# The samples' attention of a hybrid decoder step: bias by VectorE, two visits per chunk, seven value buffers

## The chip, the cores and the metric

The kernel runs on one core of a Trainium2 chip. The time is that of one execution on the device in microseconds; several executions are taken and their median is given. The profile is one more execution, recorded by the hardware profiler.

## The reference, cut to what matters

One layer of a decoder works on two groups that share all weights: a prompt of 2048 tokens, and 8 samples of 8 new tokens each, which look back at 8192 cached tokens. What matters here is the samples' attention over the cache:

```
kp = cache_k[l][page_table]          # 8 samples x 8192 tokens x 8 heads x 64
a  = lfp - reverse_cumsum(lfp)       # bias of each cached token and head
s  = q . k * scale + lq - lk         # lk = [a, lnew]
p  = softmax(where(k_pos <= q_pos, s, -inf))
o  = p . v
```

Everything is float32. The rest of the layer (projections of 8200 columns, pooling, a short convolution, the prompt's own attention, three branch products, gates, the output product, a norm) is not touched.

## The kernel before, in words

The program has three phases on TensorE. Phase 1 (`phase1`) computes all projections of the 2112 tokens: each group of 128 output columns has its weights loaded (`load_w`, line 325), split into a high and a low part (lines 326 and 327), and multiplied with the two parts of the normed input in three products for each of 8 row blocks (lines 350 to 352), in chunks of 512, 256 and 320 or 512 columns. Phase 2 is the prompt's attention, with branch products between its steps. Phase 3 is the output product.

The samples' attention (`decode`) is a Python generator that runs in the background of phase 1: after each projection chunk, `pump` takes as many steps of it as the columns done so far call for. A scheduler then orders every engine's instructions by a timeline of its own; the order of the code sets priorities. Only inside phase 2 is TensorE's order written out by hand.

Before it starts, `decode_bias` gathers the log forget values of the cache in four parts, sums them along the tokens, and stores the bias to DRAM as two arrays `s_nbh` and `s_nbl`, a high and a low part in the reduced format of TensorE's fast products. `decode_consts` makes `sel`, a matrix of zeros and ones.

A sample has 8 chunks of 8 pages (1024 tokens), 64 chunks in all. For each chunk, in four steps between which the generator yields:

1. Two loads bring the chunk's bias, `nbt`, from `s_nbh` and `s_nbl` (line 952). Two gathers bring keys, `kg` (two buffers, issued by GpSimd, line 923), and VectorE transposes them into `kt` (one buffer, line 959). Into one PSUM bank, `dS`, go two selection products, `sel` with `nbt`, which spread the bias over the rows (line 964), and on top 16 score products (line 969), each in a quarter of the columns of the array.
2. VectorE takes the maximum over both halves (line 974) and negates it (line 976); ScalarE takes the exponential and its sum (line 979); TensorE transposes the result (line 985), and ScalarE copies it to `pT` (line 988).
3. Eight products of `pT` with the first four tiles of values, `v` (line 995); the four gathers for the next tiles are put behind them (`values`, line 923).
4. Eight more with the next four tiles; VectorE masks and reduces the sum (lines 1008 and 1010).

`v` has four buffers, as many as one step uses. The first product of a step reads the tile that is gathered last:

```
with self.tc.issue_after(product(0, 3).ins):
    for x in (0, 1, 2, 4, 5, 6, 7):
        product(x // 4, x % 4)
```

GpSimd issues all gathers from one queue, and SP nearly all other transfers, both in order.

Of the kernel before, what the change touches and what calls it, by code (L numbers as in the profile page):

```python
# [8 lines left out]
F32 = mybir.dt.float32  # L9
F32R = mybir.dt.float32r  # L10
I32 = mybir.dt.int32
U32 = mybir.dt.uint32
# [6 lines left out]
P = 128  # L19
# [20 lines left out]
class Mixer:  # L40
# [5 lines left out]
    def pools(self):  # L46
# [15 lines left out]
        self.s_nbh = dt("s_nbh", [NB * NPG, NH, P])  # L62
        self.s_nbl = dt("s_nbl", [NB * NPG, NH, P])
# [3 lines left out]
    def setup(self):  # L67
# [12 lines left out]
        self.ks = self.dp.tile([P, 4, NS], F32, name="ks")  # L80
        self.vs = self.dp.tile([NS, BW], F32, name="vs")
# [772 lines left out]
    def decode_consts(self):  # L854
        nc, dp = self.nc, self.dp

        sel = self.stage("sel")[0:64, 0:256].rearrange("p (a b) -> p a b", b=P)
        self.sel = dp.tile([64, 2, P], F32R, name="sel")
        for part in range(2):
            q = slice(32 * part, 32 * part + 32)  # L860
            nc.gpsimd.iota(sel[q], pattern=[[4, 2], [1, 4], [8, 4], [0, 8]], base=0, channel_multiplier=-1,
                           allow_small_or_imprecise_dtypes=True)
        nc.vector.tensor_scalar(out=self.sel, in0=sel, scalar1=0.0, scalar2=None, op0=ALU.is_equal)

# [3 lines left out]
        for g in range(4):  # L868
# [12 lines left out]
        nc.gpsimd.affine_select(out=self.tri, in_=self.tri, pattern=[[-1, P]], compare_op=ALU.is_gt, fill=0.0,  # L881
                                base=0, channel_multiplier=1)
        nc.vector.memset(self.tri[64:128, 0:64], 0.0)

    def decode_bias(self):
# [3 lines left out]
        nc.sync.dma_start(idxl, I["page_table"].rearrange("(n b) g -> (b g) n", n=4).bitcast(U32))  # L889
# [3 lines left out]
        for n in range(4):  # L893
# [18 lines left out]
            hi, lo = self.stage(f"nbh{n}", F32R)[:, 0:1024], self.stage(f"nbl{n}", F32R)[:, 0:1024]  # L912
            nc.scalar.copy(hi, nb)
            V.tensor_tensor(out=lo, in0=nb, in1=hi.bitcast(F32), op=ALU.subtract)
            for d, x in ((self.s_nbh, hi), (self.s_nbl, lo)):
                nc.sync.dma_start(d[n * P : (n + 1) * P].rearrange("n h t -> n (h t)"), x.bitcast(F32))

    def decode(self):

# [5 lines left out]
        NC = 8  # L925

# [9 lines left out]
        vs = values(0)  # L936
        qbd = dp.tile([P, 16, 32], F32, name="qbd")
        nc.gpsimd.memset(qbd, 0.0)
        for b in range(NB):
# [6 lines left out]
            stat = dp.tile([P, 2, 2, NC], F32, tag="stat", bufs=2, name=f"stat{b}")  # L946
            ob = dp.tile([P, 2, HD, NC], F32, tag="ob", bufs=1, name=f"ob{b}")
            for c in range(NC):
# [4 lines left out]
                kt = dp.tile([P, 2, 2048], F32, tag="kt", bufs=1, name=f"kt{b}_{c}")  # L953
                for i in range(2):
                    kg = dp.tile([P, 2048], F32, tag="kg", bufs=2, name=f"kg{b}_{c}_{i}")
                    t = b * 16 + c * 2 + i
                    ind(kg, ck, self.idxk[:, t : t + 1])
                    for x in range(2):
                        V.transpose(out=kt[:, i, x * D : (x + 1) * D], in_=kg[:, x * D : (x + 1) * D])  # L959
                ktv = kt.rearrange("p i (j x r) -> p i j x r", j=4, r=32)  # L960
                S = self.psum("dS")
                Sv = S.rearrange("p (a i x) -> p a i x", a=2, x=P)
                for hh in range(2):
                    nc.tensor.matmul(Sv[:, hh], self.sel[:, hh], nbt, start=(hh == 0), stop=False)
                for hh in range(2):
                    for dh in range(2):
                        for h4 in range(4):
                            x = (4 * hh + h4) * 2 + dh
                            nc.tensor.matmul(Sv[32 * h4 : 32 * h4 + 32, hh], qbd[:, x], ktv[:, :, :, x],  # L969
                                             start=False, stop=(hh == 1 and dh == 1))  # L970
                yield
                S3 = S.rearrange("p (a x) -> p a x", a=2)
                m, l = stat[:, 0, :, c], stat[:, 1, :, c]
                V.tensor_reduce(out=m, in_=S3, axis=AX.X, op=ALU.max)
                nm = dp.tile([P, 2], F32, tag="nm", bufs=2, name=f"nm{b}_{c}")
                V.tensor_scalar(out=nm, in0=m, scalar1=-1.0, scalar2=None, op0=ALU.mult)
                pr = dp.tile([P, 2, 256], F32, tag="pr", bufs=1, name=f"pr{b}_{c}")
                for hh in range(2):
                    nc.scalar.activation(out=pr[:, hh], in_=S3[:, hh], func=AF.Exp, bias=nm[:, hh : hh + 1],
                                         accum_out=l[:, hh : hh + 1])  # L980
                pt = self.psum("dT")
                for hh in range(2):
                    for i in range(2):
                        x = hh * 2 + i
                        nc.tensor.transpose(out=pt[:, x * P : (x + 1) * P], in_=pr[:, hh, i * P : (i + 1) * P],
                                            identity=self.ident)
                pT = dp.tile([P, 4, 4, 32], F32, tag="pT", bufs=1, name=f"pT{b}_{c}")
                nc.scalar.copy(pT.rearrange("p x g (h q) -> p x h g q", q=NQ),
                               pt.rearrange("p (x h g q) -> p x h g q", x=4, h=4, g=4))
                yield  # L990
                O = self.psum("dO")
                for i in range(2):

                    def product(hh, g):
                        return nc.tensor.matmul(O[32 * g : 32 * g + 32, hh * 256 : hh * 256 + 256],  # L995
                                                pT[:, 2 * hh + i, g], vs[g][:, hh * 256 : hh * 256 + 256],
                                                start=(i == 0 and hh == 0), stop=(i == 1 and hh == 1))


                    with self.tc.issue_after(product(0, 3).ins):  # L1000
                        for x in (0, 1, 2, 4, 5, 6, 7):
                            product(x // 4, x % 4)
                    if (b * NC + c) * 2 + i + 1 < NB * NC * 2:
                        vs = values((b * NC + c) * 2 + i + 1)
                    if i == 0:
                        yield
# [577 lines left out]
```

## Time and profile before

| | us |
|---|---|
| runs before | 2932.04, 2932.24, 2920.92 (median 2932.04) |
| profiled execution | 2928.24 |
| its span, first to last instruction | 2926.5 |
| TensorE has work | 2818.0 of the span |
| VectorE, ScalarE, GpSimd | 1524.8, 771.0, 1060.9 |
| mean granted clock of TensorE | 0.981 of full speed |

Busy time counts from the start of an instruction to its modelled end. The products are pipelined, so that the distance from one start to the next, the pitch, says how fast TensorE works, and a product's own duration does not. A float32 product appears as two records. Times in the rows are microseconds from the start of the span, means are nanoseconds.

### The profile page before, as it was taken

What the parts mean: (1) busy time and instruction counts of PE and PEld (TensorE: products, weight loads), DVE (VectorE), ACT (ScalarE), POOL (GpSimd) and SP (SyncE); (2) the same over time, 40 slices, a digit from 0 to 9 for tenths busy, and PEclk for the clock granted to TensorE, in tenths of its full rate; (3) what the DMA queues carried; (4) which work ended last, traced back from release to release, by engine and by line L of the source; (5) the groups of instructions that cost most, each with busy time, mean ns of one, the idle gap of its engine ahead of it and who ended that gap; (6) DMA issues with size and microseconds to landing.
All of it is one profiled execution on the core that took longest, in us unless ns stands there. A gap on an engine that the chain in (4) does not pass through costs nothing.

```text
span 2926.5 us, 45656 instructions
## 1 busy us (share of the span) xinstructions
PE 2818.0 (96%) x17611; PEld 2162.3 (74%) x17611; DVE 1524.8 (52%) x2732; ACT 771.0 (26%) x1546; POOL 1060.9 (36%) x1210
## 2 busy tenths in 40 slices
PE   7999999999999999999999999999999999989998
PEld 4778888788878887777777777775666566758886
DVE  5465654564343345466655533226655556645554
ACT  4322221222222332222112122213333333332221
POOL 1112344453444332344444432003433343424332
PEclk9999999999999999999999999999999899989999
DMA  6776667778777867977776775624455545247542
GB/s 224 249 222 209 206 222 239 231 241 270 247 256 255 272 192 246 299 233 234 241 237 226 257 230 154 161 83 134 115 142 137 146 123 134 85 125 221 172 142 82
DMA packets 397309, 577.55 MB, mean 197 GB/s; under 512 B 45639, under 2 KB 303351, under 8 KB 377611
## 3 DMA queue, kind: packets, MB, share of 16 engines
q1 hardware_dynamic: 337123, 304.05, 36.0%
q0 software_dynamic: 59968, 270.57, 27.1%
q8 instruction: 139, 2.28, 0.3%
q14 instruction: 79, 0.65, 0.1%
HBM read 478.82 MB, written 95.60 MB: 196 GB/s over the span
## 4 chain that ended last, share of the span: by engine, by line
PE 79%; DMA 11%; DVE 3%; issue 3%; POOL 2%; ACT 1%; SPq 1%; DVEq 0%; POOLq 0%; ACTq 0%
PE ps_a L350 15%; PE ps_a L351 15%; PE ps_a L352 15%; PE ps_dO L995 4%; PE ps_dS L969 4%; PE ps_oA L1263 4%; DMA v<-in_cache_v,idxv 3%; PE ps_st L1245 3%; PE ps_mx L1170 2%; PE ps_ac L1373 2%; PE ps_ac L1372 2%; PE ps_ac L1371 2%; PE ps_st L1246 2%; DMA s_o<-oT 2%; PE ps_u L1475 1%
## 5 line engine op out<-in xcount | busy, mean ns | idle before, releaser
L350 PE MATMUL ps_a<-h,whi 128*128 128x512 f32 (+2 forms) x2560 | 921.6, 360 | 3.2 <-ACT whi L326 1.5
L351 PE MATMUL ps_a<-h,wlo 128*128 128x512 f32 (+2 forms) x2560 | 911.4, 356 | 0.9 <-DVE wlo L327 0.9
L352 PE MATMUL ps_a<-h,whi 128*128 128x512 f32 (+2 forms) x2560 | 909.7, 356 | 0.2 <-POOL h L306 0.2
L923 POOL DMA_INDIRECT v<-in_cache_v,idxv x512 | 513.9, 1004 | 735.3 <-PE ps_dO L995 593.4
L350 PEld LDWEIGHTS ps_a<-h,whi 128*128 128x128 f32 x2560 | 483.2, 189 | 99.3 <-issue 34.2
L351 PEld LDWEIGHTS ps_a<-h,wlo 128*128 128x128 f32 x2560 | 483.6, 189 | 70.0 <-issue 11.5
L352 PEld LDWEIGHTS ps_a<-h,whi 128*128 128x128 f32 x2560 | 482.9, 189 | 70.9 <-issue 10.9
L327 DVE TENSOR_TENSOR wlo<-raw,whi 128x1024 fp32r<-128x1024 f32 x128 | 160.4, 1253 | 273.7 <-ACT whi L326 273.2
L959 DVE STREAM_TRANSPOSE kt<-kg 128x1024 f32<-128x1024 f32 x256 | 296.3, 1211 | 8.3 <-DMA kg<-in_cache_k,idxk 8.1
L1173 DVE TENSOR_REDUCE mx<-ps_mx 128x1 f32<-128x512 f32 (+3 forms) x288 | 159.0, 594 | 135.4 <-PE ps_mx L1170 134.4
L1268 POOL TENSOR_TENSOR acc<-acc,pt 128x512 f32<-128x512 f32 (+2 forms) x134 | 157.9, 1178 | 148.4 <-ACT pt L1251 128.5
L1251 ACT ACTIVATE pt<-ps_st 128x512 f32<-128x512 f32 (+3 forms) x288 | 141.0, 525 | 251.8 <-PE ps_st L1246 246.1
L923 POOL DMA_INDIRECT kg<-in_cache_k,idxk x128 | 130.2, 1017 | 200.8 <-DVE kt L959 112.7
L326 ACT CAST whi<-raw 128x1024 fp32r<-128x1024 f32 x128 | 133.8, 1046 | 163.6 <-PE ps_a L352 95.2
L669 ACT ACTIVATE mg<-ps_a 128x512 f32<-128x512 f32 (+2 forms) x120 | 62.7, 522 | 401.6 <-PE ps_a L352 394.1
L1245 PEld LDWEIGHTS ps_st<-qq,kk 128*128 128x128 f32 x320 | 61.7, 193 | 134.4 <-issue 109.6
L1371 PE MATMUL ps_ac<-gh,wh 128*128 128x264 f32 x512 | 150.6, 294 | 8.8 <-ACT wh L1326 5.3
L995 PE MATMUL ps_dO<-v,pT 128*32 128x256 f32 x2048 | 146.0, 385 | 9.8 <-DMA v<-in_cache_v,idxv 9.6
L1268 DVE TENSOR_TENSOR acc<-acc,pt 128x512 f32<-128x512 f32 (+2 forms) x154 | 104.8, 683 | 90.8 <-PE ps_oB L1263 48.8
L1373 PE MATMUL ps_ac<-gl,wh 128*128 128x264 f32 x512 | 149.5, 292 | 0.5 <-DVE gl L1327 0.5
L1372 PE MATMUL ps_ac<-gh,wl 128*128 128x264 f32 x512 | 149.5, 292 | 0.1
L969 PE MATMUL ps_dS<-kt,qbd 128*32 128x256 f32 x2048 | 147.8, 386 | 0.0
(357 smaller groups left out, 4137.8 us busy)
## 6 DMA issues: line engine op xcount, KB each, us to landing
raw<-in_w_in SPq DMA_DIRECT2D x128, 512.0 KB
s_mg<-mg SPq DMA_DIRECT2D x72, 256.0 KB
t<-s_mg SPq DMA_DIRECT2D x64, 264.0 KB
x<-in_x_prompt SPq DMA_DIRECT2D x32, 512.0 KB
s_m<-t SPq DMA_DIRECT2D x64, 132.0 KB
wc<-in_w_cond SPq DMA_DIRECT2D x16, 512.0 KB
v<-in_cache_v,idxv POOLq DMA_INDIRECT x512, 4.7
m<-s_m SPq DMA_DIRECT2D x64, 128.0 KB
```

What stands on the lines that cost most here:

```text
L327: nc.vector.tensor_tensor(out=lo, in0=raw, in1=hi.bitcast(F32), op=ALU.subtract)
L350: nc.tensor.matmul(acc, whi[:, k], hh, start=(k == 0), stop=False)
L351: nc.tensor.matmul(acc, wlo[:, k], hh, start=False, stop=False)
L352: nc.tensor.matmul(acc, whi[:, k], hl, start=False, stop=(k == KT - 1))
L923: ind = lambda out, src, idx: nc.gpsimd.indirect_dma_start(out=out, out_offset=None, in_=src, in_offset=bass.IndirectOffsetOnAxis(ap=idx, ...
L959: V.transpose(out=kt[:, i, x * D : (x + 1) * D], in_=kg[:, x * D : (x + 1) * D])
L969: nc.tensor.matmul(Sv[32 * h4 : 32 * h4 + 32, hh], qbd[:, x], ktv[:, :, :, x], start=False, stop=(hh == 1 and dh == 1))
L995: return nc.tensor.matmul(O[32 * g : 32 * g + 32, hh * 256 : hh * 256 + 256], pT[:, 2 * hh + i, g], vs[g][:, hh * 256 : hh * 256 + 256], s ...
L1268: e.tensor_tensor(out=acc[h, Q][:, lo:512], in0=acc[h, Q][:, lo:512], in1=pt[:, lo:512], op=ALU.add)
L1371: nc.tensor.matmul(y, wh[:, k, cols], hi[:, k], start=(k == 0), stop=False)
L1372: nc.tensor.matmul(y, wl[:, k, cols], hi[:, k], start=False, stop=False)
L1373: nc.tensor.matmul(y, wh[:, k, cols], lo[:, k], start=False, stop=(k == 3))
```

## The change

The bias is stored once, in float32, as `s_nb`, in the order in which a chunk's score rows need it. The selection products and `sel` go. Four loads per chunk, each with a broadcast over a sample's 8 queries, fill a tile `nbt` of 128 partitions (one buffer). VectorE adds it to the scores in PSUM and takes the maximum in the same instruction, one for each half (line 986 after). The four steps of a chunk become two visits, which run one chunk apart in a pipeline: the first holds the first eight value products of chunk k-1 and, tied behind them, the scores of chunk k; the second holds the other eight value products of chunk k-1 and, tied behind them, the transposes of chunk k's exponentials. `v` has seven buffers. To make room, the samples' new keys and values share a buffer with `ob`, and the result of the new tokens is stored to DRAM (`s_no`) and read back at the end.

```diff
-            hi, lo = self.stage(f"nbh{n}", F32R)[:, 0:1024], self.stage(f"nbl{n}", F32R)[:, 0:1024]
-            nc.scalar.copy(hi, nb)
-            V.tensor_tensor(out=lo, in0=nb, in1=hi.bitcast(F32), op=ALU.subtract)
-            for d, x in ((self.s_nbh, hi), (self.s_nbl, lo)):
-                nc.sync.dma_start(d[n * P : (n + 1) * P].rearrange("n h t -> n (h t)"), x.bitcast(F32))
+            dst = self.s_nb[16 * n : 16 * n + 16].rearrange("c g h (a i x) -> i a (c g) h x", a=2, i=2)
+            for i in range(2):
+                for a in range(2):
+                    src = nb[64 * i : 64 * i + 64, 512 * a : 512 * a + 512]
+                    nc.sync.dma_start(dst[i, a], src.rearrange("p (h x) -> p h x", h=4))
...
-                nbt = dp.tile([64, 2, P], F32R, tag="nbt", bufs=2, name=f"nbt{b}_{c}")
-                for part, d in ((0, self.s_nbh), (1, self.s_nbl)):
-                    src = d[b * NPG + 8 * c : b * NPG + 8 * c + 8].rearrange("(t g) h x -> (g h) t x", g=4)
-                    nc.sync.dma_start(nbt[32 * part : 32 * part + 32].bitcast(F32), src)
+            nbt = dp.tile([P, 2, 256], F32, tag="nbt", bufs=1, name=f"nbt{k}")
+            for h4 in range(4):
+                nc.sync.dma_start(nbt[32 * h4 : 32 * h4 + 32].rearrange("p a x -> p (a x)"),
+                                  self.s_nb[k, :, h4].unsqueeze(1).broadcast_to([4, NQ, 4 * P]))
...
-                for hh in range(2):
-                    nc.tensor.matmul(Sv[:, hh], self.sel[:, hh], nbt, start=(hh == 0), stop=False)
...
-                V.tensor_reduce(out=m, in_=S3, axis=AX.X, op=ALU.max)
+            for hh in range(2):
+                V.tensor_tensor_reduce(out=S3[:, hh], in0=S3[:, hh], in1=nbt[:, hh], scale=1.0, scalar=-3 * BIG,
+                                       op0=ALU.add, op1=ALU.max, accum_out=m[:, hh : hh + 1])
...
+            with self.tc.issue_after(product(0, 3).ins):
+                for x in (0, 1, 2, 4, 5, 6, 7):
+                    last = product(x // 4, x % 4)
+            with self.tc.issue_after(last.ins):
+                then()
+            return values(2 * k + i + 1) if 2 * k + i + 1 < NB * NC * 2 else None
...
+        for k in range(n + 1):
+            run = lambda: None
+            if k < n:
+                S, nbt, run = scores(k)
+            if k:
+                O = self.psum("dO")
+                vs = products(k - 1, 0, pT, O, vs, run)
+            else:
+                run()
             yield
+            nxt = []
+            if k < n:
+                pr = softmax(k, S, nbt)
+                run = lambda: nxt.append(transposes(k, pr))
+            else:
+                run = lambda: nxt.append(None)
+            if k:
+                vs = products(k - 1, 1, pT, O, vs, run)
+                evict(k - 1, O)
+            else:
+                run()
+            pT = nxt[0]
+            yield
+            if k and k % NC == 0:
+                sequence(k // NC - 1)
+                yield
...
-    DECODE_STEPS = NB * (8 * 4 + 1) + 4
+    DECODE_STEPS = 2 * (NB * 8 + 1) + NB + 4
...
-    m.st_bufs, m.sc_bufs, m.v_bufs, m.pt_bufs, m.raw_bufs = 4, 8, 4, 5, 1
+    m.st_bufs, m.sc_bufs, m.v_bufs, m.pt_bufs, m.raw_bufs = 4, 8, 7, 5, 1
```

TensorE, before, the scores of one chunk and the value products of the chunk ahead, which the scheduler put into the same place (outputs `ps_dS` are scores, `ps_dO` value products; x2 means two such instructions in a row):

```order
L964 MATMUL ps_dS<-nbt_3_3072,sel 128x256 x2
L969 MATMUL ps_dS<-kt_3_3075,qbd 32x256
L995 MATMUL ps_dO<-v_3_2980,pT_2_2928 32x256
L995 MATMUL ps_dO<-v_0_2974,pT_2_2928 32x256
L995 MATMUL ps_dO<-v_1_2976,pT_2_2928 32x256
L995 MATMUL ps_dO<-v_2_2978,pT_2_2928 32x256
L995 MATMUL ps_dO<-v_0_2974,pT_2_2928 32x256
L995 MATMUL ps_dO<-v_1_2976,pT_2_2928 32x256
L995 MATMUL ps_dO<-v_2_2978,pT_2_2928 32x256
L995 MATMUL ps_dO<-v_3_2980,pT_2_2928 32x256
L969 MATMUL ps_dS<-kt_3_3075,qbd 32x256 x15
```

TensorE, after, a first visit:

```order
L1011 MATMUL ps_dO<-v_3_3383,pT_3375 32x256
L1011 MATMUL ps_dO<-v_0_3377,pT_3375 32x256
L1011 MATMUL ps_dO<-v_1_3379,pT_3375 32x256
L1011 MATMUL ps_dO<-v_2_3381,pT_3375 32x256
L1011 MATMUL ps_dO<-v_0_3377,pT_3375 32x256
L1011 MATMUL ps_dO<-v_1_3379,pT_3375 32x256
L1011 MATMUL ps_dO<-v_2_3381,pT_3375 32x256
L1011 MATMUL ps_dO<-v_3_3383,pT_3375 32x256
L977 MATMUL ps_dS<-kt_3454,qbd 32x256 x16
```

The selection products are gone, and all scores stand behind the value products. Counted over the whole order, blocks of score and value products are entered from another kind of product 174 times before and 152 times after.

GpSimd, before, the gathers of one chunk (`v` values, `kg` keys):

```order
L923 DMA v_0_6526<-in_cache_v,idxv 128x512
L923 DMA v_1_6528<-in_cache_v,idxv 128x512
L923 DMA v_2_6530<-in_cache_v,idxv 128x512
L923 DMA v_3_6532<-in_cache_v,idxv 128x512
L923 DMA kg_5_0_7057<-in_cache_k,idxk 128x2048
L923 DMA kg_5_1_7061<-in_cache_k,idxk 128x2048
L923 DMA v_0_6603<-in_cache_v,idxv 128x512
L923 DMA v_1_6605<-in_cache_v,idxv 128x512
L923 DMA v_2_6607<-in_cache_v,idxv 128x512
L923 DMA v_3_6609<-in_cache_v,idxv 128x512
```

GpSimd, after, the same:

```order
L928 DMA v_0_6665<-in_cache_v,idxv 128x512
L928 DMA v_1_6667<-in_cache_v,idxv 128x512
L928 DMA v_2_6669<-in_cache_v,idxv 128x512
L928 DMA kg_0_6951<-in_cache_k,idxk 128x2048
L928 DMA kg_1_6955<-in_cache_k,idxk 128x2048
L928 DMA v_3_6671<-in_cache_v,idxv 128x512
L928 DMA v_0_6782<-in_cache_v,idxv 128x512
L928 DMA v_1_6784<-in_cache_v,idxv 128x512
L928 DMA v_2_6786<-in_cache_v,idxv 128x512
L928 DMA v_3_6788<-in_cache_v,idxv 128x512
```

Before, all four tiles of a step stand behind the two gathers of keys; after, three of the four stand ahead of them, and the last, `v_3`, behind.

## Rows read from the trace of the kernel before

**Rows 1.** The page's first part: engine, busy us (share), instructions.

```profile
PE 2818.0 (96%) x17611; PEld 2162.3 (74%) x17611; DVE 1524.8 (52%) x2732; ACT 771.0 (26%) x1546; POOL 1060.9 (36%) x1210
```

**Rows 2.** Busy time by window: TensorE, weight loads, VectorE, ScalarE, GpSimd, clock, DMA share, GB/s.

```profile
600.00:700.00 100.00, 100.00 (x786) 81.00 (x785) 52.12 (x64) 21.60 (x48) 47.58 (x47) 1.00 0.75 243
900.00:1000.00 100.00, 99.03 (x756) 80.59 (x755) 40.84 (x52) 24.43 (x60) 44.20 (x45) 1.00 0.80 259
```

**Rows 3.** TensorE's timeline, 640 to 672 us: start, duration, line, operation, shape, records.

```profile
648.41 0.38 PE L964 MATMUL ps_dS<-nbt,sel 64*128 64x256 f32 x1
...
658.90 0.28 PE L350 MATMUL ps_a<-h,whi 128*128 128x256 f32 x1
659.02 0.28 PE L351 MATMUL ps_a<-h,wlo 128*128 128x256 f32 x1
659.23 1.07 PE L995 MATMUL ps_dO<-v,pT 128*32 128x256 f32 x16
660.23 0.39 PE L352 MATMUL ps_a<-h,whi 128*128 128x256 f32 x1
660.45 0.28 PE L350 MATMUL ps_a<-h,whi 128*128 128x256 f32 x1
...
670.50 0.39 PE L351 MATMUL ps_a<-h,wlo 128*128 128x512 f32 x1
670.72 0.39 PE L352 MATMUL ps_a<-h,whi 128*128 128x512 f32 x1
671.04 0.50 PE L964 MATMUL ps_dS<-nbt,sel 64*128 64x256 f32 x2
671.47 0.41 PE L969 MATMUL ps_dS<-kt,qbd 128*32 128x256 f32 x2
```

**Rows 4.** TensorE's waits: who waited for what, us in total, times, longest.

```profile
PE ps_dO L995 <- DMA v<-in_cache_v,idxv: 9.6, 13, 1.8
PE ps_mx L1170 <- DMA k<-s_nlkh: 6.6, 1, 6.6
PE ps_tr L906 <- DVE t L905: 4.7, 3, 2.5
```

**Rows 5.** TensorE's timeline at one such wait (in brackets: idle before, and releaser).

```profile
1673.64 1.49 PE L969 MATMUL ps_dS<-kt,qbd 128*32 128x256 f32 x20
1676.89 1.07 PE L995 MATMUL ps_dO<-v,pT 128*32 128x256 f32 x16 [1.76 <-DMA v<-in_cache_v,idxv]
```

**Rows 6.** VectorE's groups by shape: count, busy us, mean ns of one, idle before.

```profile
L974 DVE TENSOR_REDUCE stat<-ps_dS 128x2 f32<-128x512 f32 x64 | 44.2, 690 | 91.8 <-PE ps_dS L969 91.4
...
L1175 DVE CUSTOM_DVE_ANT_0 ps_mx<-ps_mx,causal 128x128 f32<-128x128 f32 x128 | 36.8, 296 | 14.5 <-PE ps_mx L1170 13.6
...
L1175 DVE DVE_READ_ACCUMULATOR2_ANT mx<- 128x1 f32 x128 | 17.9, 140 | 0.0
```

**Rows 7.** VectorE's timeline behind the scores that end near 652 us.

```profile
652.03 0.69 DVE L974 TENSOR_REDUCE stat<-ps_dS 128x2 f32<-128x512 f32 x1 [0.89 <-PE ps_dS L969]
652.64 4.61 DVE L959 STREAM_TRANSPOSE kt<-kg 128x1024 f32<-128x1024 f32 x4
657.18 0.13 DVE L976 TENSOR_SCALAR nm<-stat 128x2 f32<-128x2 f32 x1
```

**Rows 8.** DMA, 300 to 1750 us: packets, MB, share; issues, KB, median us to landing.

```profile
q0 software_dynamic: 54963, 248.18, 49.9%
q1 hardware_dynamic: 158258, 102.86, 24.1%
...
v<-in_cache_v,idxv POOLq DMA_INDIRECT x474, 4.8
...
nbt<-s_nbh SPq DMA_DIRECT2D x59, 32.0 KB
...
kg<-in_cache_k,idxk POOLq DMA_INDIRECT x118, 7.8
```

More of the change, by code (lines that the diff above doesn't have):

```diff
@@ L855, in decode_consts @@
         nc, dp = self.nc, self.dp
[L857 to L863, printed above, removed]
         om = self.stage("om")[:, 0:4]
@@ L925, in decode @@
         NC = 8
+        qbd = dp.tile([P, 16, 32], F32, name="qbd")
+        nc.gpsimd.memset(qbd, 0.0)
+        seq = {}
         def values(x):
@@ L934, in values, with queries @@
             return vs
[L936 to L939, printed above, removed]
+        def queries(b):
             qv = qbd.rearrange("p (f a) c -> p f a c", a=4)
@@ new lines, in queries, with scores, run @@
+            seq[b] = (dp.tile([P, 2, 2, NC], F32, tag="stat", bufs=2, name=f"stat{b}"),
+                      dp.tile([P, 2, HD, NC], F32, tag="ob", bufs=1, name=f"ob{b}"))
+        def scores(k):
+            b, c = divmod(k, NC)
+            if c == 0:
+                queries(b)
+            nbt = dp.tile([P, 2, 256], F32, tag="nbt", bufs=1, name=f"nbt{k}")
+            for h4 in range(4):
+                nc.sync.dma_start(nbt[32 * h4 : 32 * h4 + 32].rearrange("p a x -> p (a x)"),
+                                  self.s_nb[k, :, h4].unsqueeze(1).broadcast_to([4, NQ, 4 * P]))
+            kt = dp.tile([P, 2, 2048], F32, tag="kt", bufs=1, name=f"kt{k}")
+            for i in range(2):
+                kg = dp.tile([P, 2048], F32, tag="kg", bufs=2, name=f"kg{k}_{i}")
+                ind(kg, ck, self.idxk[:, 2 * k + i : 2 * k + i + 1])
+                for x in range(2):
+                    V.transpose(out=kt[:, i, x * D : (x + 1) * D], in_=kg[:, x * D : (x + 1) * D])
+            ktv = kt.rearrange("p i (j x r) -> p i j x r", j=4, r=32)
+            S = self.psum("dS")
+            Sv = S.rearrange("p (a i x) -> p a i x", a=2, x=P)
+            def run():
@@ L977, in decode @@
[L977 to L991, printed above, removed]
-                for i in range(2):
[L994 to L1006, printed above, removed]
@@ L1007, in decode @@
[L1007 to L1011 removed]
+                                             start=(hh == 0 and dh == 0), stop=(hh == 1 and dh == 1))
@@ new lines, in scores, with softmax @@
+            return S, nbt, run
+        def softmax(k, S, nbt):
+            stat, c = seq[k // NC][0], k % NC
+            S3 = S.rearrange("p (a x) -> p a x", a=2)
+            m, l = stat[:, 0, :, c], stat[:, 1, :, c]
+            for hh in range(2):
+                V.tensor_tensor_reduce(out=S3[:, hh], in0=S3[:, hh], in1=nbt[:, hh], scale=1.0, scalar=-3 * BIG,
+                                       op0=ALU.add, op1=ALU.max, accum_out=m[:, hh : hh + 1])
+            nm = dp.tile([P, 2], F32, tag="nm", bufs=2, name=f"nm{k}")
+            V.tensor_scalar(out=nm, in0=m, scalar1=-1.0, scalar2=None, op0=ALU.mult)
+            pr = dp.tile([P, 2, 256], F32, tag="pr", bufs=1, name=f"pr{k}")
+            for hh in range(2):
+                nc.scalar.activation(out=pr[:, hh], in_=S3[:, hh], func=AF.Exp, bias=nm[:, hh : hh + 1],
+                                     accum_out=l[:, hh : hh + 1])
+            return pr
@@ new lines, in transposes @@
+        def transposes(k, pr):
+            pt = self.psum("dT")
+            for hh in range(2):
+                for i in range(2):
+                    x = hh * 2 + i
+                    nc.tensor.transpose(out=pt[:, x * P : (x + 1) * P], in_=pr[:, hh, i * P : (i + 1) * P],
+                                        identity=self.ident)
+            pT = dp.tile([P, 4, 4, 32], F32, tag="pT", bufs=1, name=f"pT{k}")
+            nc.scalar.copy(pT.rearrange("p x g (h q) -> p x h g q", q=NQ),
+                           pt.rearrange("p (x h g q) -> p x h g q", x=4, h=4, g=4))
+            return pT
@@ new lines, in products, with product @@
+        def products(k, i, pT, O, vs, then):
+            def product(hh, g):
+                return nc.tensor.matmul(O[32 * g : 32 * g + 32, hh * 256 : hh * 256 + 256],
+                                        pT[:, 2 * hh + i, g], vs[g][:, hh * 256 : hh * 256 + 256],
+                                        start=(i == 0 and hh == 0), stop=(i == 1 and hh == 1))
+            with self.tc.issue_after(product(0, 3).ins):
[4 more added lines that the diff above has]
+            return values(2 * k + i + 1) if 2 * k + i + 1 < NB * NC * 2 else None
```

67 lines of the change are left out of this document (32 added, 35 removed).

## The prediction

> **What bounds the kernel now.** I read the page's busy line first, then busy time per 100 us, then TensorE's own timeline, then who waits for whom, and last the DMA view. The busy line has TensorE at 96% of the span and every other engine at 52% or less [rows 1]. That alone says little, since a busy TensorE is not one at its peak, so the stretch in which the samples' attention runs is looked at by itself: between 300 and 1750 us TensorE has work in 99% and more of a window, at a granted clock of 1.00, while VectorE stands at 41 to 52% and the DMA engines at 75 to 80% [rows 2]. In the timeline the projections follow each other at a fixed pitch, 0.22 us from one 512-column product to the next and 0.12 us for 256 columns [rows 3]; they never run dry. So in this stretch the end is set by the sum of TensorE's work. The samples' attention (64 chunks, one each 22.6 us: 671.04 less 648.41 [rows 3]) is put between the projections, and each tenth of a microsecond that it takes less on TensorE, per chunk, is 6.4 us of the span. What can hide such a gain is only a later wait of TensorE itself.
>
> **The change part by part.** The profiled execution took 2928.24 us (span 2926.5), 3.8 us under the median of the three runs, 2932.04. The sum is made against 2928.24.
>
> *Selection products.* Two products per chunk go (L964, 128 in all). In 59 of the 64 chunks they stand next to each other in the order, and the trace shows such a pair from 671.04 to the first score product at 671.47: 0.43 us [rows 3]. The entry into the samples' block ahead of them stays: the first row after the projection at 670.72 begins 0.10 us later than the pitch of 0.22 would have it, and the score products then meet that entry themselves. 64 x 0.43 = 27.5 us. The other five pairs are split by products with the values; I count them alike. Nothing hides this work, TensorE is the engine that is full; it is the safest term.
>
> *Two visits per chunk.* A visit costs an entry and an exit. The products with the values at 659.23 begin 0.21 us after the last projection's start at 659.02, where the pitch of 256 columns is 0.12 (659.02 less 658.90): 0.09 us in. The second row behind them comes 0.22 us after the first (660.45 less 660.23) instead of 0.12: 0.10 us out. Together 0.19 us [rows 3]. The scheduler already merges some blocks before. Counted in the two orders of TensorE, blocks of score and value products that are entered from something else number 174 before and 152 after, not 128 as two visits per chunk would give, since single projections and transposes still fall in between. 22 x 0.19 = 4.2 us.
>
> *Waits for values.* TensorE waited 13 times for a gathered tile of values, 9.6 us in all [rows 4]; one of them reads: score products from 1673.64, then 1.76 us idle until the tile landed, then the products at 1676.89 [rows 5]. A gather lands a median 4.8 us after its issue [rows 8]; with four buffers none of the next four tiles can be asked for before the products of this visit let go of theirs, with seven three of the four are asked for a visit, some 11 us, earlier. The fourth, which the first product needs, still waits for a buffer of this visit, and stands on GpSimd's queue behind two gathers of keys, each of which lands after 7.8 us [rows 8]. Gain between 0 and 9.6; I take 8, since before, in every other visit, all four tiles stood behind the keys and 115 of 128 visits still did not wait.
>
> *VectorE adds the bias.* Out goes a maximum over 128x512 of 690 ns; in come two adds with a maximum over 128x256. This form stands in the trace over 128x128, 296 ns and 140 ns for reading its accumulator [rows 6]. Twice as wide it costs between once and twice that, 0.44 to 0.87 us, so 0.2 to 1.05 us more per chunk, 12 to 67 us of VectorE over the phase. VectorE has about half of its time free there [rows 2], so it costs the end nothing; if that cover were gone, all of it would show. The chain from scores to exponentials gets longer by the same amount. Its length now: the maximum begins at 652.03, four transposes of keys follow on VectorE, and the negated maximum comes at 657.18 [rows 7]. After the change VectorE's order puts those four transposes between the two adds. Even with 1 us more this ends some 7 us after the scores; the second visit, which holds the transposes of the exponentials, comes about 11 us (half of 22.6) after the first. I take 0, with 0 to 0.5 us per chunk as the bound.
>
> *Bias tiles.* The two loads of 32 KB per chunk [rows 8] become four with 64 KB each, on SP's queue, and the tile has one buffer, so that SP waits with the next load for VectorE's adds of this chunk; the loads of projection weights and the stores of gates queue behind that. It is asked for a chunk ahead of its use. The added 192 KB x 64 = 12.6 MB take, at the 24.1% of 16 engines over 1450 us that 102.86 MB took on this queue (54 us of one engine per MB, an estimate), 680 us of one engine, 43 us spread over 16, 3% of the stretch. With DMA at 75 to 80% this is covered, if it spreads (second rival).
>
> *Preparation.* The split of the bias in two parts goes and scattered stores come, in the first 250 us. TensorE waited 4.7 us there for the sums [rows 4]; this could go or grow by as much. I take 0. The new values' result by way of DRAM and the shared buffer for keys and values are outside TensorE's path: 0.
>
> Sum: 27.5 + 4.2 + 8 = 39.7, so 2928 - 40 = **2888 us**, 1.4% less. Bounds of the terms: without the 8 us 2896; with all 9.6 and the 4.7 of the preparation 2882.
>
> **The rivals.**
> 1. *The exponentials come late to the second visit.* Their transposes on TensorE are now tied to stand behind the products with values; if the adds, the four transposes of keys and the two exponentials do not fit in 11 us, TensorE stops with everything behind it. For: VectorE's order has the key transposes inside this chain, and they wait for a gather. Against: about 4 us of slack by the rows. Price: the bound of 0.5 us in each of 64 chunks, 32 us, and the time would be 2928 - 40 + 32 = 2920, no change that can be told.
> 2. *The bias loads crowd a few DMA engines* (slower than before). Each of the four loads reads four rows, each for eight partitions. If a load is not spread over 16 engines but over four, and all loads over the same four, these carry 256 KB per chunk: at 47 to 54 us per MB [rows 8] 12 to 14 us of one engine, 3.1 to 3.5 us on each of four in every 22.6 us, 14 to 15% on top of 75 to 80%, which is 90 to 95%. A gather is complete when its slowest part is, so tiles of keys, values and projection weights would land later, and TensorE would wait for them. It turns the result from 40/64 = 0.62 us of new waits per chunk on; with 1 us per chunk it gives 2928 - 40 + 64 = 2952. For: the share is high already. Against: the seven value buffers and the two of keys ask a visit or a chunk ahead. The Trainium skill has such a rule ("DMA: Bandwidth & Descriptors", Rules for kernel authors: a DMA whose outermost dimension has c < 16 entries is confined to at most c engines); no row of before shows a load of this shape in the stretch, so the rule is neither borne out nor refuted here, and by it this rival's first condition would hold while its second, that the crowding reaches TensorE, stays open.
> 3. *The waits for values stay*, since the first product needs the tile that is asked for last: 2896.
> 4. *More goes than counted.* The waits of the preparation go (4.7 us), and the 6.6 us for which TensorE stands still at the first product of the prompt's maxima [rows 4], because the samples' attention ends earlier: 2888 - 11 = 2877.
>
> That the change does not do what it says can be seen from the order in part: the selection products are gone, the visits are merged only from 174 to 152.
>
> **How the numbers follow.** Chances: forecast (2880 to 2893) 0.56; rival 3 0.14; rival 4 0.11; rival 1 0.12; rival 2 0.07. What a measurement of this kernel can tell from no change is about 0.5%, 15 us, so below 2917 is faster. Forecast, rivals 3 and 4 are faster: 0.81. Rival 1 is within: 0.12. Rival 2 is slower: 0.07. The range holds the forecast and rivals 3 and 4 with the 6 us by which the three runs differ, and a part of rival 1: 2868 to 2914.
>
> **What would show it.** In the profile after: no row of a selection product, and the phase's last projection some 40 us earlier; the pitch of the projections unchanged; TensorE's waits for values near 2 us. Rival 1 would show as TensorE waiting for the exponentials, rival 2 as longer landing times of gathers and TensorE waiting for keys, values or weights, rival 3 as the old wait for values. The forecast is wrong if the stretch's TensorE has idle time of more than some 20 us between 300 and 1750.

## The result, and the profile after

The changed kernel took 2897.89 us, median of four runs (2893.58 to 2900.21), beside 2928.64 us for the kernel before: a ratio of 0.9897, interval 0.9871 to 0.9923. That is 30.7 us less; 40 less, 2888, was forecast. The median lies beside the third rival's 2896. The two profiled executions differ by 34.7 us (2928.24 to 2893.58, span 2891.9).

The busy line of the changed kernel's page, and the two windows of [rows 2] in its trace:

```profile
PE 2781.9 (96%) x17483; PEld 2145.3 (74%) x17483; DVE 1525.1 (53%) x2919; ACT 768.0 (27%) x1543; POOL 1065.7 (37%) x1211
```

```profile
600.00:700.00 100.00, 100.00 (x796) 82.62 (x796) 52.10 (x81) 22.25 (x47) 46.62 (x48) 1.00 0.81 264
900.00:1000.00 100.00, 98.55 (x788) 82.30 (x789) 46.30 (x71) 24.33 (x58) 41.98 (x44) 1.00 0.85 276
```

TensorE has 128 rows fewer, the selection products, and is as full as before [rows 1, 2]. The DMA share has risen from 0.75 and 0.80 to 0.81 and 0.85. VectorE's groups of the new add, 300 to 1750 us (count, busy us, mean ns, idle before):

```profile
L986 DVE CUSTOM_DVE_ANT_0 ps_dS<-ps_dS,nbt 128x256 f32<-128x256 f32 x122 | 50.7, 416 | 134.1 <-DMA nbt<-s_nb 64.6 <-PE ps_dS L977 52.5 <-DMA s_mg<-mg 6.7
L986 DVE DVE_READ_ACCUMULATOR2_ANT stat<- 128x1 f32 x122 | 16.4, 134 | 0.2
```

One add costs 416 ns and 134 for reading its accumulator, in the lower half of the forecast's bounds [rows 6]. The whole stretch of 300 to 1750 us in the kernel before and in the changed kernel, read as in [rows 2]:

```profile
300.00:1750.00 1450.00, 1440.23 (x10156) 1124.33 (x10156) 752.54 (x1012) 340.20 (x737) 628.05 (x620) 1.00 0.74 243
300.00:1750.00 1450.00, 1436.63 (x10252) 1131.78 (x10251) 773.88 (x1239) 353.55 (x753) 642.23 (x637) 1.00 0.80 256
```

TensorE stands idle for 9.8 us of it before and 13.4 after, under the 20 that the prediction set.

TensorE's timeline at a merged visit and at the prompt's first score product, which ends the phase:

```profile
801.11 0.39 PE L355 MATMUL ps_a<-h,whi 128*128 128x512 f32 x1
801.42 1.07 PE L1011 MATMUL ps_dO<-v,pT 128*32 128x256 f32 x16
802.31 1.91 PE L977 MATMUL ps_dS<-kt,qbd 128*32 128x256 f32 x32
804.15 0.38 PE L353 MATMUL ps_a<-h,whi 128*128 128x256 f32 x1
...
1929.06 0.39 PE L1296 MATMUL ps_st<-qq,kk 128*128 128x512 f32 x1
```

VectorE's timeline behind that visit:

```profile
804.29 0.43 DVE L986 CUSTOM_DVE_ANT_0 ps_dS<-ps_dS,nbt 128x256 f32<-128x256 f32 x1 [5.60 <-PE ps_dS L977]
```

The same end of the phase in the kernel before:

```profile
1966.42 0.39 PE L1245 MATMUL ps_st<-qq,kk 128*128 128x512 f32 x1
```

The phase ends 37.4 us earlier; the rest of the span gave back 2.7 us. A visit is now one row of products, and the add starts 0.07 us after the last score product (802.31 + 1.91 = 804.22).

TensorE's waits in the changed kernel (us in all, times, longest):

```profile
PE ps_dO L1011 <- DMA v<-in_cache_v,idxv: 10.0, 11, 2.5
...
PE ps_mx L1221 <- DMA k<-s_nlkl: 4.1, 1, 4.1
```

The bias tile's loads in its trace (ns of an issue, least, median and most), and its DMA queues, both 300 to 1750 us:

```profile
L960 SPq DMA_DIRECT2D nbt<-s_nb x240: 597/604/5350, 310.6 to 1672.7; - x120
```

```profile
q0 software_dynamic: 56137, 252.00, 51.9%
q1 hardware_dynamic: 161634, 118.06, 27.7%
```

The waits for values did not go: 10.0 us after 9.6 [rows 4]. One of them, 2.5 us, lies ahead of 300 us and is new; from 300 us on they are 7.5 us after 9.6. The wait for the keys of the maxima fell from 6.6 to 4.1 us, and the wait for the sums of the preparation is no longer among TensorE's. The queue of loads and stores moved 15.2 MB more in the stretch and took 3.6% more of the 16 engines [rows 8], about what was forecast for the bias tiles.

### The profile page after: what moved, and what is told of

Same layout as the page of the kernel before. It is cut to its first block, busy times and chain, and to the rows that moved or that the text cites. A ratio compares the mean times of both kernels' runs of the same rounds, so it can differ in the third digit from the quotient of the medians.

```text
span 2891.9 us, 45880 instructions
## 1 busy us (share of the span) xinstructions
PE 2781.9 (96%) x17483; PEld 2145.3 (74%) x17483; DVE 1525.1 (53%) x2919; ACT 768.0 (27%) x1543; POOL 1065.7 (37%) x1211
## 4 chain that ended last, share of the span: by engine, by line
PE 72%; DMA 12%; DVE 4%; issue 3%; POOL 2%; ACT 1%; SPq 1%; DVEq 0%; POOLq 0%; ACTq 0%
PE ps_a L353 14%; PE ps_a L354 13%; PE ps_a L355 13%; PE ps_dO L1011 4%; PE ps_oA L1314 4%; PE ps_dS L977 4%; DMA v<-in_cache_v,idxv 3%; PE ps_st L1296 3%; DMA raw<-in_w_in 2%; PE ps_mx L1221 2%; PE ps_ac L1424 2%; PE ps_ac L1423 2%; PE ps_ac L1422 2%; PE ps_st L1297 2%; DMA s_o<-oT 2%
## 5 line engine op out<-in xcount | busy, mean ns | idle before, releaser
L1314 PE MATMUL ps_oA<-pt,vh 128*64 128x512 f32 (+3 forms) x288 | 140.0, 569 | 1.1 <-POOL pt L1304 1.1
```

What stands on the lines that cost most here:

```text
L1314: nc.tensor.matmul(O[s][64 * s : 64 * s + 64, lo:512], v[:, kt], pt[:, lo:512], start=(kt == 0), stop=(kt == 4 * Q + 3))
```

## The experiments

Twelve runs were made, four to a batch. Each batch ran on a chip of its own, and its runs of the kernel before are shared within it; a time is compared inside its batch, or by its ratio to the kernel before.

### First batch: one part alone, one part taken out

**The kernel before without its selection products**

```diff
-                for hh in range(2):
-                    nc.tensor.matmul(Sv[:, hh], self.sel[:, hh], nbt, start=(hh == 0), stop=False)
...
-                                             start=False, stop=(hh == 1 and dh == 1))
+                                             start=(hh == 0 and dh == 0), stop=(hh == 1 and dh == 1))
```

> The kernel before without its 128 selection products (the bias is then left out of the scores; its loads stay). Theory: the samples' stretch is bound by the sum of TensorE's work, so the whole 0.43 us per chunk comes off the end: 27.5 us less than before, about 2901 us against 2928.6. Rival: part of it is taken back by a later wait of TensorE, mostly for values, since a shorter stretch asks for the same gathers sooner: 15 to 20 us less, about 2911.

2924.86 us, ratio 0.9972 (0.9957 to 0.9987): 9 us less by the medians, not 27, and less than the rival's 15 to 20. TensorE's waits of this kernel between 300 and 1980 us:

```profile
PE ps_dO L993 <- DMA v<-in_cache_v,idxv: 20.7, 23, 2.0
...
PE ps_dO L993 <- ACT pT L986: 4.7, 1, 4.7
```

The waits for values are twice those of [rows 4], and TensorE's idle time from 300 us to the phase's end is 32.2 us instead of 16.4. The reading is that with four buffers the work that was taken away had covered gathers that were late anyway. It is not shown free of the chip: the trace of the kernel before is not from this batch.

**The changed kernel with four buffers of values**

```diff
-    m.st_bufs, m.sc_bufs, m.v_bufs, m.pt_bufs, m.raw_bufs = 4, 8, 7, 5, 1
+    m.st_bufs, m.sc_bufs, m.v_bufs, m.pt_bufs, m.raw_bufs = 4, 8, 4, 5, 1
```

> The changed kernel with four buffers of values instead of seven. Theory (the last tile decides: with seven buffers, too, the first product waits for a tile that is asked for only when this visit's buffers come free): TensorE's waits for values stay near the 10 us that seven buffers have, and the time within 5 us of the changed kernel, 2898. Rival (the three early tiles count, and the new loads only hide it): waits for values of 20 us and more, 2910 or more.

2986.41 us, ratio 1.0176 (1.0152 to 1.0201): 52 us slower than the kernel before, as the rival had it, and by more. TensorE's waits over its whole run:

```profile
PE ps_dO L1011 <- DMA v<-in_cache_v,idxv: 79.0, 32, 9.8
```

The same for 900 to 1200 us alone, and the busy times of that window:

```profile
PE ps_dO L1011 <- DMA v<-in_cache_v,idxv: 53.3, 10, 9.8
```

```profile
900.00:1200.00 300.00, 237.01 (x1653) 184.95 (x1652) 109.40 (x181) 71.66 (x147) 108.50 (x108) 0.86 0.66 216
```

The changed kernel's window, with seven buffers:

```profile
900.00:1200.00 300.00, 293.76 (x1998) 232.24 (x1999) 151.25 (x248) 92.24 (x188) 109.30 (x108) 1.00 0.79 257
```

TensorE's timeline with four:

```profile
1084.21 1.94 PE L1011 MATMUL ps_dO<-v,pT 128*32 128x256 f32 x16 [9.81 <-DMA v<-in_cache_v,idxv]
1085.89 2.54 PE L977 MATMUL ps_dS<-kt,qbd 128*32 128x256 f32 x32
1093.53 1.93 PE L1011 MATMUL ps_dO<-v,pT 128*32 128x256 f32 x16 [5.10 <-DMA v<-in_cache_v,idxv]
```

Between the two halves of the prompt's rows projections run out, and this order has eight visits nearly side by side from 1062 to 1139 us. With four buffers each must first let go of its tiles before the next can be asked for, so seven of the eight wait out a gather. TensorE stands idle for 7.7 us ahead of the first of them, and from 1056 to 1145 us the granted clock is for the most part at half, 1.2 of 2.4 GHz; over the window it is 0.86. A row of sixteen value products then takes 1.94 us, and not 1.07. The order is planned anew for the four buffers, so this is not the changed order with a wait added; but this order, with merged visits and four buffers, is slower than the kernel before.

**One load of sixteen rows for the bias tile, in place of four of four rows**

```diff
-                    src = nb[64 * i : 64 * i + 64, 512 * a : 512 * a + 512]
-                    nc.sync.dma_start(dst[i, a], src.rearrange("p (h x) -> p h x", h=4))
+                    for g in range(4):
+                        src = nb[64 * i + g : 64 * i + 64 : 4, 512 * a : 512 * a + 512]
+                        nc.sync.dma_start(dst[i, a, g], src.rearrange("p (h x) -> p h x", h=4))
...
-            for h4 in range(4):
-                nc.sync.dma_start(nbt[32 * h4 : 32 * h4 + 32].rearrange("p a x -> p (a x)"),
-                                  self.s_nb[k, :, h4].unsqueeze(1).broadcast_to([4, NQ, 4 * P]))
+            nc.sync.dma_start(nbt.rearrange("p a x -> p (a x)"),
+                              self.s_nb[k].rearrange("h g x -> (h g) x").unsqueeze(1).broadcast_to([16, NQ, 4 * P]))
```

> The changed kernel with the bias kept in another order in DRAM, so that one load with 16 rows in its outermost dimension fills the tile, in place of four loads with 4 rows each. The same bytes. Theory A (the four-row loads crowd a few DMA engines and bring back the wait for values): waits for values fall from 10 us to 3 or less and VectorE's 64.6 us of waiting for the bias falls to under 20; 2898 - 8 = 2890 us. Theory B (the wait for values comes from the last tile's place behind the keys): waits for values stay near 10 us, the time within 4 us of 2898.

2926.41 us, ratio 0.998 (0.9966 to 0.9995). Both theories missed the time, and not over the load: each store of the preparation became four, 64 in all on SyncE's queue. TensorE's waits between 190 and 310 us, here:

```profile
PE ps_tr L435 <- DVE nat L426: 10.9, 2, 10.4
PE ps_tr L425 <- DVE chist L697: 5.9, 1, 5.9
```

and in the changed kernel:

```profile
PE ps_tr L435 <- DVE nat L426: 0.4, 1, 0.4
```

The first products with values come at 255.6 us instead of 223.3. So the time says nothing on the load; the third batch mends it. Of theory A's two signs one came: no add waited for its bias tile any more, but TensorE still waited 12.4 us for values, 9.4 of them from 300 us on.

**The changed kernel with the bias tile loaded once**

> The changed kernel with the bias tile loaded for the first chunk alone (all others use the first chunk's bias); VectorE's adds stay. Theory A: no bias traffic, so waits for values at 3 us or less and the time 2888 to 2892. Theory B: the loads cost the end nothing, waits for values near 10 us, 2894 to 2902.

2888.52 us, ratio 0.9848 (0.9823 to 0.9874), waits for values 4.7 us: theory A's time, with a little more waiting than it had. Beside 0.9897 that is 14 us for the loads, across chips; the third batch measures it on one.

### Second batch: parts put back, and the same kernel again

**The changed kernel, unaltered**

> The changed kernel as it is, beside the others of this batch on the same chip. Both theories: the ratio to the kernel before that it had, 0.9897 (0.987 to 0.992), about 30 us less; it is the base for the runs with parts put back or taken out.

2931.38 us (12 runs, 2925.76 to 2942.33), ratio 0.9982 (0.9967 to 0.9997). The same kernel, with the same instructions in the same order on TensorE, gained 6 us here and not 31. TensorE's row and VectorE's at the chunk shown above:

```profile
819.33 1.91 PE L977 MATMUL ps_dS<-kt,qbd 128*32 128x256 f32 x32
```

```profile
824.08 0.43 DVE L986 CUSTOM_DVE_ANT_0 ps_dS<-ps_dS,nbt 128x256 f32<-128x256 f32 x1 [7.17 <-remote]
```

TensorE's waits:

```profile
PE ps_dO L1011 <- DMA v<-in_cache_v,idxv: 20.8, 18, 2.4
...
PE ps_dT L1001 <- ACT pr L992: 6.7, 10, 1.4
```

GpSimd's wait for a key tile's buffer, in the first trace of the changed kernel:

```profile
POOL kg L928 <- DVE kt L967: 164.0, 87, 28.4
```

and in this one:

```profile
POOL kg L928 <- DVE kt L967: 270.9, 104, 28.5
```

The scores end at 821.24, VectorE stands idle, and the add starts at 824.08: 2.84 us instead of 0.07. The key transposes stand between the two adds on VectorE, so they are late too, GpSimd waits longer to ask for the next keys, and the gathers of values stand behind that on its queue. TensorE waits 20.8 us for values, and 6.7 us for exponentials, which the first trace has at 0.4; its idle time from 300 us to the phase's end is 39.6 us instead of 17.5. That is 22 of the 35 us between the two profiled executions. The chain is read from the waits; no run takes the lateness away. Why the add hears so late I did not find; the last section has what the traces show.

**The kernel before with six buffers, and without selection products with seven.** Both take the change's way of making room (new keys and values in the buffer of the sequence's result, the new values' result by way of DRAM); the second leaves the bias out.

```diff
-    m.st_bufs, m.sc_bufs, m.v_bufs, m.pt_bufs, m.raw_bufs = 4, 8, 4, 5, 1
+    m.st_bufs, m.sc_bufs, m.v_bufs, m.pt_bufs, m.raw_bufs = 4, 8, 6, 5, 1
```

> The kernel before with its selection products and its visits, and six buffers of values instead of four (room made as the change makes it: the new keys and values in the buffer of the sequence's result, the new values' result by way of DRAM). Ledger theory (the terms of the sum add up one by one): only the 9.6 us of waits for values can go, so 5 to 9 us less than before, ratio 0.997 to 0.998. Slack theory (TensorE's selection work already covered most of the gathers; buffers pay only where that work is gone): nothing, ratio 0.999 to 1.001, waits for values from 9.6 to under 5 us but as much elsewhere.

> The kernel before without the 128 selection products (the bias is left out) and with seven buffers of values; visits as before. Its partner is the same kernel with four buffers, 0.9972 and 21.4 us of waits for values. Slack theory: with the waits covered the 27.5 us come through, ratio 0.989 to 0.991, the waits for values under 10 us: then the two visits are worth nothing. Visits theory (the gain hangs on the two visits per chunk, which space the products evenly): it stays at 0.995 to 0.998.

2925.89 us, ratio 0.9959 (0.9945 to 0.9973), and 2927.39 us, ratio 0.996 (0.9944 to 0.9976). TensorE's wait for values in the first:

```profile
PE ps_dO L997 <- DMA v<-in_cache_v,idxv: 9.6, 9, 2.3
```

That is as much as with four buffers [rows 4], though the kernel is 11 us faster by the medians. Neither theory fits: by the medians the time fell by more than either had, and not by way of these waits. Where it came from stays open, since no trace of the kernel before was taken on this chip. TensorE's waits of the second, from 300 us on:

```profile
PE ps_dO L987 <- DMA v<-in_cache_v,idxv: 2.1, 3, 1.4
```

and between 100 and 300 us:

```profile
PE ps_a L352 <- ACT z L412: 8.4, 1, 8.4
PE ps_tr L1065 <- DVE npT L1061: 6.8, 1, 6.8
```

With seven buffers and no selection products the waits for values are 2.1 us, after 20.7 with four, on a schedule whose visits stand apart. (The two ran in different batches, and six buffers beside the selection products took nothing off.) The time does not show it, since this order loses 15.2 us in two waits of the preparation that the other kernels don't have. By 300 us it has done 110 projection products fewer than the kernel before, some 24 us at a pitch of 0.22, and makes up for them by the phase's end (1966.7 us after 1966.4): about what the selection products took there. So what the two visits are worth by themselves is not told by this pair.

**The selection's work put back into the changed kernel**, as products of zeros with zeros:

```diff
             def run():
+                for hh in range(2):
+                    nc.tensor.matmul(Sv[:, hh], self.zz, self.zz.unsqueeze(1).broadcast_to([64, 2, P]), start=(hh == 0), stop=False)
```

> The changed kernel with two products per chunk of the old selection's shape (64 rows, 128x256, zeros times zeros, into the scores' bank ahead of the score products); the bias still comes from VectorE. Ledger theory: 64 x 0.43 us = 27.5 us more than the changed kernel, ratio 0.998 to 1.000. Slack theory: as much, since the changed kernel has buffers enough to be bound by TensorE's work. Rival (the products lie in waits, as the -9 us of taking them out of the kernel before suggest): 5 to 12 us more, ratio 0.992 to 0.994.

2974.61 us, ratio 1.013 (1.0104 to 1.0156): 43 us more than the unaltered kernel of the batch, more than any theory said. TensorE's timeline:

```profile
654.43 1.07 PE L1017 MATMUL ps_dO<-v,pT 128*32 128x256 f32 x16
655.43 0.50 PE L978 MATMUL ps_dS<-zz 64*128 64x256 f32 x2
655.86 1.93 PE L983 MATMUL ps_dS<-kt,qbd 128*32 128x256 f32 x32
```

The pair takes 0.43 us, as in [rows 3]. But it stands between products with values and scores, and the sixteen products take 1.00 us to the next row instead of 0.89 (801.42 to 802.31). 64 x 0.54 = 35 us. Of the other 8, 2.6 us are more idle time from 300 us to the phase's end (42.2 after 39.6), and some 5 lie in a slower preparation, with 22 projection products fewer by 300 us. With seven buffers the products cost their time in full.

### Third batch: what the bias loads do

> The changed kernel as it is, a third time, as the base of this batch on one chip. Its first measurement gave a ratio of 0.9897 to the kernel before, its second, in another batch, 0.9982, with the same order of instructions on every engine. If the first was the rule, 0.990 here; if the chip of the batch decides, anything between.

> The changed kernel with one load of sixteen rows per chunk for the bias tile instead of four loads of four rows, and the stores of the preparation, four times as many and a quarter as large, put in turn on ScalarE's and SyncE's queues (all on SyncE's, they had held TensorE up by some 30 us ahead of the first values). Crowding theory (four loads of four rows each sit on a few DMA engines and hold up gathers, weights and the bias itself): 25 to 40 us less than the changed kernel of this batch, and TensorE's waits between 300 us and the phase's end 14 to 22 us instead of 47. Queue theory (SyncE's queue waits with the next load for VectorE's adds, and the weights behind it are late): the same time as the changed kernel, since the load still waits for the one buffer.

> The changed kernel with the bias tile loaded only for the first chunk (the other 63 add the same tile, so the samples' attention is computed with a wrong bias), beside the changed kernel on the same chip. Both theories of the loads: 25 to 45 us less than the changed kernel of this batch. Rival (the chip of the batch made the difference between 0.985 here and 0.998 there): within 8 us of it.

> The changed kernel with two buffers for the bias tile, and six instead of seven for the values to make room: the loads of a chunk no longer wait for the adds of the chunk before, so nothing on SyncE's queue stands behind that wait. Queue theory: 25 to 40 us less than the changed kernel of this batch. Crowding theory: within 8 us of it, since the same four loads are issued.

The edits are those of the first batch's one load and no loads, with

```diff
-                        nc.sync.dma_start(dst[i, a, g], src.rearrange("p (h x) -> p h x", h=4))
+                        (nc.sync if g % 2 else nc.scalar).dma_start(dst[i, a, g], src.rearrange("p (h x) -> p h x", h=4))
```

for the former, and for the two bias buffers bufs=2 at the tile and six buffers of values. The kernel before stood at 2923.95 us. "Waits for values" is TensorE's, 300 to 1980 us; "add waits for the tile" is VectorE's, 300 to 1750 us; "TensorE idle" is all its idle time from 300 us to the phase's end.

| kernel | median us | ratio (95%) | waits for values | add waits for the tile | TensorE idle |
|---|---|---|---|---|---|
| changed kernel | 2890.77 | 0.9874 (0.9853 to 0.9896) | 5.4 us, 7 times | 60.7 us, 12 times | 16.2 us |
| one load of sixteen rows | 2890.72 | 0.9884 (0.9865 to 0.9904) | 2.1 us, 3 times | none | 8.4 us |
| no loads | 2878.56 | 0.9852 (0.9831 to 0.9872) | 0.4 us, once | none | 5.0 us |
| two bias buffers | 2894.89 | 0.9895 (0.9875 to 0.9914) | 8.8 us, 12 times | none | 17.7 us |

TensorE's wait for values and what VectorE's adds waited for longest (us, times), in the changed kernel:

```profile
PE ps_dO L1011 <- DMA v<-in_cache_v,idxv: 5.4, 7, 1.1
```

```profile
  DMA nbt<-s_nb: 60.7, 12
```

with one load of sixteen rows:

```profile
PE ps_dO L1011 <- DMA v<-in_cache_v,idxv: 2.1, 3, 0.9
```

```profile
  PE ps_dS L977: 142.5, 40
```

without the loads:

```profile
PE ps_dO L1013 <- DMA v<-in_cache_v,idxv: 0.4, 1, 0.4
```

and with two bias buffers:

```profile
PE ps_dO L1011 <- DMA v<-in_cache_v,idxv: 8.8, 12, 2.3
```

```profile
  PE ps_dS L977: 138.8, 33
```

The gathers of values between 300 and 1750 us (count, median us from issue to landing), in the changed kernel, with one load, and without loads:

```profile
v<-in_cache_v,idxv POOLq DMA_INDIRECT x491, 6.0
v<-in_cache_v,idxv POOLq DMA_INDIRECT x489, 5.4
v<-in_cache_v,idxv POOLq DMA_INDIRECT x489, 4.6
```

The first measurement repeats: 0.9874 here, 0.9897 there. Both theories were sized at 25 to 40 us, by what the second batch's chip had lost, and no run here gains that. The queue theory has no row for it either: with two bias buffers the adds no longer wait for their tile, and the time is the same or 4 us more, though this run also has one buffer of values fewer; and with one load SyncE's queue stands at the load as long as with four (348 and 344 us), while TensorE's idle time is half.

Without the loads TensorE hardly waits for values, and the kernel takes 12 us less by the medians, 6 by the ratios, whose intervals overlap. The idle time, 16.2 us with the loads and 5.0 without, gives 11: this is about their price. With the same bytes as one load of sixteen rows the adds find their tile, a gather lands sooner, and TensorE's idle time falls by 7.8 us. The time is not less: this order idles 6.4 us more ahead of 300 us (32.3 after 25.9) and has 1657 rows of TensorE done by then against 1697. So the loads cost what they cost by slowing the gathers, which the landing times show, and not by holding up SyncE's queue. In the stretch itself the other shape saved most of it in this trace; a saving in the whole time is not shown.

## Why the prediction was right, and where it was not

**The bound** was right: TensorE is as full as before and what it no longer does shows at the phase's end.

**Selection products** (27.5 us) held, as far as a sum over rows can tell. From 300 us to the phase's end the stretch is 37.4 us shorter, and TensorE's idle time in it is the same (16.4 and 17.5 us over all rows). 61 of the chunks lie in it, 61 x 0.43 = 26. The products put back cost 0.43 us a pair again. What the forecast did not say is that this needs the buffers: taken alone, with four buffers, only 9 us came off the end on the first batch's chip, and TensorE's idle time rose by 16.

**Two visits** (4.2 us): in that stretch the blocks of the samples' products are entered 140 times instead of 165, 25 x 0.19 = 4.8 us. Ten projections more were done by 300 us, 2 us. Of the 37.4 us some 5 remain that I can't give to a row.

**Waits for values** (8 us) is the term that failed: 10.0 us are left of 9.6, as in the third rival. Its reason was another, though: without the bias loads the last-asked tile is still the first one needed, and in the third batch 0.4 us is left. The step that failed stands in the part on the bias tiles: "this is covered, if it spreads". With the loads a gather of values lands after 6.0 us, without them after 4.6, and TensorE waits 5.4 us instead of 0.4: the loads put back what seven buffers can take. That is the second rival's mechanism, with the sign it named, at a tenth to a fifth of its price: it was sized at 64 us, 1 us per chunk, and measured 6 to 12 us in all. On the first batch's chip, where the adds start late, 4.7 us of waits are left even without the loads, so they are not the whole of it there. The rule of the Trainium skill that was named there ("DMA: Bandwidth & Descriptors", Rules for kernel authors: fewer than 16 entries outermost keep a transfer on at most that many engines) is not contradicted by the one load's rows, with no late bias tile, 2.1 us of waits and gathers that land after 5.4 us at equal bytes; but two buffers also did away with the late tiles, one load is also one transfer in place of four, and no trace shows which engine carried a packet, so the rule stays unproved here.

**VectorE** was right: 773.9 us busy between 300 and 1750 against 752.5, 0.35 us a chunk, and nothing behind it late where the signal comes at once: 0.4 us of waiting for exponentials. On the second batch's chip the first rival came true in part, 6.7 us.

**Preparation** was put at 0, and held: the 4.7 us of waits for the sums went, as in the fourth rival, while others came (2.5 us for the first values among them), and TensorE's idle time up to 300 us is 23.0 us after 23.4.

So 40 us less was forecast and 34.7 measured between the profiled executions: 8 that stayed and 2.7 that the later phases gave back, against some 6 more than counted, mostly the part that I can't give to a row and the products done by 300 us. That the sum came so near is in part luck: a term that failed was met by gains that no one had counted. What was not foreseen at all is that on another chip the gain shrank to 6 us: 2931 there lies outside the range of 2868 to 2914. There six buffers alone (11 us) or the products alone with seven buffers (10 us) gave at least as much as the whole change.

## What to carry to other kernels

Work that is taken from a full engine may be worth less than its time unless what arrives beside it arrives earlier as well: with four buffers 9 of the 27 us came through, and merged visits with four buffers were slower than before. A transfer that "is covered" by its bytes can still slow the gathers for which the full engine waits, here from 4.6 to 6.0 us; price it by leaving it out once. And measure a change of one per cent on more than one chip: the same program gave 0.987, 0.990 and 0.998.

## What was not expected of the hardware

In the traces of the first measurement and of the third batch, VectorE starts 0.07 us after the last score product where that is what it stood idle for. In those of the first two batches it mostly starts late. The figures are medians over the chunks ahead of which VectorE was idle, 300 to 1650 us. In the second batch it is 2.9 us in the unaltered kernel, 3.7 with the products of zeros, and 1.5 and 1.6 in the two kernels whose visits are apart. In the first it is 2.05 us in the kernel without loads, 2.7 with one load, 1.3 with four buffers, and 1.0 in the one whose visits are apart. By the median, what follows projections (0.04 to 0.07 us), transposes of exponentials (0.09) and products with values (0.15) is about as prompt in all traces looked at. Within the second batch the lateness grew with the row of narrow products, 128x32, ahead of the signal; in the first, kernels with the same rows differ by twice, and the first trace and the third batch have the same rows and no lateness.

Lateness alone did not take the gain: without loads the kernel stood at 0.985 on the first batch's chip, with its adds 2.05 us late, and on the third's, with none late. On the second batch's chip the kernel before took 2937 us, 13 more than on the third's, and the changed kernel 41 more; there the adds are late and the loads are there as well. Whether it is the chip, and what in it, no run here tells: that stays open.
